# Moving the row scaling of the final norm to the end of the last expert, and the last down-projection block in two halves

## The chip, the cores and the metric

The kernel runs on one NeuronCore of a Trainium2 chip, as one program. The metric is the time of one execution on the device in microseconds (us). TensorE multiplies matrices into PSUM, VectorE and ScalarE work on tiles in SBUF and PSUM, GpSimd (POOL in the profile) does small operations and issues the indirect transfers, SyncE (SP) issues the plain transfers. A matmul in float32 precision is made of float32r products: each operand is split into a rounded high half and the low rest.

## The reference, cut to what matters

One layer of a diffusion backbone over 1024 latent tokens of 1024 channels. The change lies in its last part, a mixture of 16 experts and the final norm:

```
def expert_choice_ffn(h, w_router, w_gate, w_up, w_down):
    ...
    gates, idx = lax.top_k(jnp.swapaxes(aff, 1, 2), cap)      # cap = 128 tokens of each of 16 experts
    xe = jax.vmap(lambda hb, ib: hb[ib])(h, idx)
    hid = jax.nn.silu(jnp.einsum('becd,edf->becf', xe, w_gate)) * jnp.einsum('becd,edf->becf', xe, w_up)
    ye = jnp.einsum('becf,efd->becd', hid, w_down) * gates[..., None].astype(h.dtype)
    return jax.vmap(lambda yb, ib: jnp.zeros((n, d), yb.dtype).at[ib.reshape(-1)].add(yb.reshape(-1, d)))(ye, idx)
...
        x = x + gt2 * expert_choice_ffn(h, router_w[i], exp_w_gate[i], exp_w_up[i], exp_w_down[i])
    return rms_norm(x, final_g)
```

The root mean square of a token's row is taken over all its 1024 channels, so a row can be scaled only when every expert that chose the token has added to it.

## The kernel before, in words

The experts run one after the other. Each has 24 weight blocks of 512 by 512 (1 MB of float32): blocks 0 to 15 are gate and up (four hidden blocks of 512 channels, four weight blocks each), blocks 16 to 23 are the down projection, in the order of `DOWN` (L1214), (n2, kk) = (0,0), (0,1), (0,2), (1,0), (1,1), (1,2), (0,3), (1,3): n2 is the half of the 1024 output channels, kk the hidden block. So block 21 is (1,2), block 22 completes the first half of the output and block 23 the second.

`Stream.get` (L121) keeps weights ahead of the products: at block b it emits the split of block b+2. A split (L75, L76) is a cast of the raw block on ScalarE (`ewh`) and a subtraction on VectorE (`ewl`); the last two blocks are split in quarters of 512 columns. Three pairs of `ewh` and `ewl` exist, so the cast of block b+3 waits for the products of block b with its `ewh`. A block is 12 products of 512 columns: eight with `ewh`, four with `ewl` (`products`, L83).

PE, ScalarE and VectorE run in the order in which the program is written (`tc.manual_schedule`, L1714); SP and POOL are ordered by the framework. In that order block b does: the split of block b+2, the list `pre[b]`, the list `post[b]`, its products. What the lists hold for the last expert, whose block 0 is L:

- `hidden` (L1636), per hidden block: silu on ScalarE, multiply into `sge` on VectorE, four transposes on TensorE, and the split of the transposed block (`hd`: copy on ScalarE, subtraction on VectorE). For the last hidden block: silu in post 14, multiply in post 16, transposes in pre 18, split in post 18.
- `rows` (L1674, post 1) loads all 1024 rows of the residual stream as eight tiles of 128 tokens, once the scatter of the last but one expert is done. They hold every contribution but the last expert's.
- `row_sum(t)` (L1686, post 11+t): squares and sum of tile t on ScalarE; for every second t the reciprocal root for two tiles on POOL (`rstd_of`, L201).
- `row_out(t)` (L1692): VectorE scales tile t by the reciprocal root and the norm's weight `fg`, SP writes it to `out`. It stands in post 13, 14, 16, 17, 19, 20, 21 and 22.
- `last_rows(n2)` (L1696), for the 128 tokens of the last expert: the down projection's half times gate and `gt2` (`yl`), added to their rows (`xl`), squares summed on ScalarE (`ssl`), and times `fg` (`zl`). `last_rows(0)` stands in post 23, `last_rows(1)` behind block 23.

After the loop: the two sums added, the reciprocal root (L749, one step of it on POOL), `zl` scaled by it, the first half on VectorE and the second on ScalarE (L1751, L1752), and an indirect DMA on POOL's queue that scatters these 128 rows into `out` (L1753), over what `row_out` wrote for the same tokens.

Of the kernel before, what the change touches and what calls it, by code (L numbers as in the profile page):

```python
# [8 lines left out]
F32 = mybir.dt.float32  # L9
# [5 lines left out]
AF = mybir.ActivationFunctionType  # L15
OP = mybir.AluOpType
AX = mybir.AxisListType

D = 1024
# [8 lines left out]
NE = 16  # L28
CAP = 128
DE = 2048  # L30
EPS = 1e-6
# [4 lines left out]
def block_kernel(ctx: ExitStack, tc, x, c, cx, c_ctx, w_ada, b_ada, norm1_g, norm2_g, w_in, w_a_up, b_a,  # L36
# [3 lines left out]
    V, S, G, T = nc.vector, nc.scalar, nc.gpsimd, nc.tensor  # L40
# [18 lines left out]
    small = ctx.enter_context(tc.tile_pool(name="small", bufs=2))  # L59
# [11 lines left out]
    def ps(name="ps"):  # L71
        return psum.tile([128, 512], F32, name=name, tag="ps")
# [10 lines left out]
    def products(p, ab, w, first, last, again=False):  # L83

        seq = [q for a, b in ab for q in ((a[0], b[0]), (a[0], b[1]) if w == 0 else (a[1], b[0]))]
        seq += [(a[1], b[0]) if w == 0 else (a[0], b[1]) for a, b in ab]
        for i, (a, b) in enumerate(seq):
            T.matmul(p, a, b, start=first and i == 0, stop=last and i == len(seq) - 1, skip_group_check=again)  # L88
            yield

    def mmw(p, ab, w=0, first=True, last=True, again=False):
        for _ in products(p, ab, w, first, last, again):
            pass

    def drain(gen, n=None):

        i = 0
        while n is None or i < n:
            try:
                next(gen)  # L100
            except StopIteration:
                return True
            i += 1
        return False
# [93 lines left out]
    mhalf = const.tile([128, 8], F32, name="mhalf")  # L198
    V.memset(mhalf, -0.5)

    def rstd_of(dst, ssq, n, cols, eng=None):  # L201

        a = small.tile([128, cols], F32, name="rs_a", tag="rs_a", bufs=4)
        r = small.tile([128, cols], F32, name="rs_r", tag="rs_r", bufs=4)
        t = small.tile([128, cols], F32, name="rs_t", tag="rs_t", bufs=4)
        eng = eng or V
        eng.tensor_scalar(a, ssq, 1.0 / n, EPS, op0=OP.mult, op1=OP.add)  # L207
        G.tensor_tensor(r, a, mhalf[:, :cols], op=OP.pow)  # L208
        eng.tensor_mul(t, r, r)  # L209
        eng.tensor_mul(t, t, a)  # L210
        eng.tensor_scalar(t, t, -0.5, 1.5, op0=OP.mult, op1=OP.add)  # L211
        eng.tensor_mul(dst, r, t)  # L212
# [52 lines left out]
    def g4(name, dt=F32):  # L265
        return gw.tile([128, N], dt, name=name, tag="g4", bufs=GB)
# [78 lines left out]
    def ada_mm(j):  # L345
        p = ps()
        for k in range(KT):
            q = 32 * (k % 4)
            T.matmul(p[q:q + 32, :256], cS32[:, k], pairs[j][:, k], start=(k < 4), stop=(k >= 4))
        a = hpool.tile([128, 256], F32, name="ada", tag="A", bufs=2)  # L350
        V.tensor_copy(a, p[:, :256])
        return a
# [43 lines left out]
    xl, xl2 = [], []  # L396
    pv = [[ps() for hf in range(2)] for t in range(2)]
    plr = ps()
    for j in range(KT):
# [8 lines left out]
        if j + 1 < KT:  # L408
            a = ada_mm(j + 1)
        w = ws.get()  # L410
        for t in range(2):
            st = (hcT[j][0][:, t * 128:(t + 1) * 128], hcT[j][1][:, t * 128:(t + 1) * 128])
# [383 lines left out]
    for h in range(H):  # L796
# [33 lines left out]
        o = [g4("o0"), g4("o1")]  # L830
# [16 lines left out]
    for i in range(2):  # L847
        w = ws.get()
# [303 lines left out]
    for j in range(8):  # L1152
        w = ws.get()
# [32 lines left out]
    for f in range(2):  # L1186
# [3 lines left out]
        for j in range(8):  # L1190
            w = ws.get()
# [7 lines left out]
            hi, lo = mgX[j // 4][f]  # L1199
# [303 lines left out]
    while not drain(sg_, 1):  # L1503
# [27 lines left out]
                           op0=OP.add, op1=OP.mult)  # L1531
# [74 lines left out]
    gt2 = ep.tile([128, D], F32, name="gt2")  # L1606

    def spread(dst, c0):

        for n in range(2):  # L1610
            dg = ep.tile([128, 4, 128], F32, name="dg", tag="oh", bufs=1)
            for k in range(4):
                S.activation(dg[:, k], ident, AF.Copy, scale=mc[:, c0 + 4 * n + k:c0 + 4 * n + k + 1])
            yield
            p = ps()
            for k in range(4):
                T.matmul(p[:, k * 128:(k + 1) * 128], ones, dg[:, k], start=True, stop=True)
            yield
            S.copy(dst[:, n * 512:(n + 1) * 512], p)
# [7 lines left out]
    NB = 24  # L1627
    pre = [[] for _ in range(NE * NB + 2)]
    post = [[] for _ in range(NE * NB + 2)]

    def put(gen, *places):

        for where, b in places:
            where[b].append(lambda: drain(gen, 1))
# [33 lines left out]

    lt = {}
    ssq = small.tile([128, 8], F32, name="ssq3", bufs=1)  # L1670
    ssl = small.tile([128, 2], F32, name="ssl", bufs=1)
    rs = small.tile([128, 8], F32, name="rs3", bufs=1)

    def rows():  # L1674
# [11 lines left out]
    def row_sum(t):  # L1686
        sq = ep.tile([128, D], BF16, name="sq3", tag="oh", bufs=1)
        S.activation(sq, xs[t], AF.Square, accum_out=ssq[:, t:t + 1])  # L1688
        if t % 2:
            rstd_of(rs[:, t - 1:t + 1], ssq[:, t - 1:t + 1], D, 2, G)  # L1690

    def row_out(t):  # L1692
        V.scalar_tensor_tensor(xs[t], xs[t], rs[:, t:t + 1], lt["fg"], op0=OP.mult, op1=OP.mult)
        nc.sync.dma_start(out[t * 128:(t + 1) * 128, :], xs[t])

    def last_rows(n2, st):  # L1696

        gate, xl, zl, fg = tok[NE - 1][2], lt["xl"], lt["zl"], lt["fg"]
        h = slice(n2 * 512, (n2 + 1) * 512)
        yl = ep.tile([128, 512], F32, name="yl", tag="sge", bufs=2)  # L1700
        sq = ep.tile([128, 512], F32, name="sq4", tag="sge", bufs=2)
        V.scalar_tensor_tensor(yl, st["pd", n2], gate, gt2[:, h], op0=OP.mult, op1=OP.mult)
        V.tensor_tensor(xl[:, h], xl[:, h], yl, op=OP.add)
        S.activation(sq, xl[:, h], AF.Square, accum_out=ssl[:, n2:n2 + 1])
        V.tensor_tensor(zl[:, h], xl[:, h], fg[:, h], op=OP.mult)

    L = (NE - 1) * NB
    post[L + 1].append(rows)
    for t in range(8):
        post[L + 11 + t].append(lambda t=t: row_sum(t))  # L1710
        post[L + (13, 14, 16, 17, 19, 20, 21, 22)[t]].append(lambda t=t: row_out(t))
    put(spread(gt2, 16), (post, 9), (pre, 11), (post, 12), (pre, 14), (post, 15))

    with tc.manual_schedule(engines={mybir.EngineType.PE, mybir.EngineType.Activation, mybir.EngineType.DVE}):  # L1714
        for g in range(NE * NB):
            e, b = divmod(g, NB)
            if b == 0:
                st = {}
                for nb in range(4):
                    put(hidden(e, nb, st), (post, g + 4 * nb + 2), (post, g + 4 * nb + 4), (pre, g + 4 * nb + 6),  # L1720
                        (post, g + 4 * nb + 6))
                if e + 1 < NE:
                    put(gather(e + 1), (post, g + 4), (pre, g + 6), (post, g + 7))
                    pre[g + 17].append(lambda e=e: lt.update(ei=expert_in(e + 1)))
                    for w_, b_ in ((pre, 17), (post, 17), (pre, 20), (post, 20)):
                        w_[g + b_].append(lambda: drain(lt["ei"], 1))
                    put(expert_out(e, st), (post, g + 23), (post, g + 24))
                else:
                    post[g + 23].append(lambda st=st: last_rows(0, st))
            w = es.get()  # L1730
            for f in pre[g] + post[g]:
                f()
            if b < 16:
                nb, r = divmod(b, 4)
                nm = "pu" if r > 1 else "pg", nb
                if r % 2 == 0:
                    st[nm] = ps()
                mmw(st[nm], [(xT[e](4 * (r % 2) + k), w(k)) for k in range(4)], 1, r % 2 == 0, r % 2 == 1)
            else:
                n2, kk = DOWN[b - 16]  # L1740
                if kk == 0:
                    st["pd", n2] = ps()
                hi, lo = st["hd", kk]
                mmw(st["pd", n2], [((hi[:, k * 128:(k + 1) * 128], lo[:, k * 128:(k + 1) * 128]), w(k)) for k in range(4)],
                    1, kk == 0, kk == 3)
        last_rows(1, st)
    rl = small.tile([128, 1], F32, name="rl", bufs=1)
    V.tensor_add(ssl[:, 0:1], ssl[:, 0:1], ssl[:, 1:2])
    rstd_of(rl, ssl[:, 0:1], D, 1)
    zl = lt["zl"]  # L1750
    V.tensor_scalar(zl[:, :512], zl[:, :512], rl, None, op0=OP.mult)  # L1751
    S.activation(zl[:, 512:], zl[:, 512:], AF.Copy, scale=rl)  # L1752
    nc.gpsimd.indirect_dma_start(out=out[:, :], out_offset=bass.IndirectOffsetOnAxis(ap=tok[NE - 1][0][:, :1], axis=0),  # L1753
                                 in_=zl, in_offset=None)
    close(epc)
# [28 lines left out]
```

## Time and profile before

| | |
|---|---|
| time, median of 3 runs | 2319.63 us (2318.67 to 2321.66) |
| the profiled execution | 2319.61 us, its span 2317.8 us |
| TensorE busy | 2243.7 us, 97% of the span |
| VectorE busy | 1734.1 us, 75% |
| ScalarE busy | 1341.3 us, 58% |
| mean granted TensorE clock | 0.988 |

All times in rows are us from the start of the span. In a time line a row has start, duration, engine, line, operation, out<-in and the number of operations merged into it; in square brackets the idle time of the engine before it and what ended it. L75, L76 and L88 are lines of helpers, so the tile names tell the operation. In rows of groups the mean duration of one operation, in ns, stands behind the bar after the busy time. `eraw` is the name of all tiles of the weight ring; the rows of tokens and `zl` lie in such tiles too.

### The profile page before, as it was taken

What the parts mean: (1) busy time and instruction counts of PE and PEld (TensorE: products, weight loads), DVE (VectorE), ACT (ScalarE), POOL (GpSimd) and SP (SyncE); (2) the same over time, 40 slices, a digit from 0 to 9 for tenths busy, and PEclk for the clock granted to TensorE, in tenths of its full rate; (3) what the DMA queues carried; (4) which work ended last, traced back from release to release, by engine and by line L of the source; (5) the groups of instructions that cost most, each with busy time, mean ns of one, the idle gap of its engine ahead of it and who ended that gap; (6) DMA issues with size and microseconds to landing.
All of it is one profiled execution on the core that took longest, in us unless ns stands there. A gap on an engine that the chain in (4) does not pass through costs nothing. (4 is left out here: it accounts for less than half of the span.)

```text
span 2317.8 us, 28964 instructions
## 1 busy us (share of the span) xinstructions
PE 2243.7 (97%) x10930; PEld 1861.4 (80%) x10930; DVE 1734.1 (75%) x2183; ACT 1341.3 (58%) x1538; POOL 281.8 (12%) x388
## 2 busy tenths in 40 slices
PE   6999999999999999999959999999999999999997
PEld 4888888888788887888748888888888888888885
DVE  5764545454866665476688999999999999999988
ACT  3743433342333344253448777777777777777786
POOL 1201010101000023320210111100011101011104
PEclk9999999999999999999979999999999999999998
DMA  9423333334222258665579999999999999999995
GB/s 321 157 61 110 103 107 99 109 96 155 64 75 76 77 180 264 215 204 180 221 281 324 388 383 380 375 380 393 392 386 376 380 376 393 388 388 378 382 349 208
DMA packets 356341, 589.60 MB, mean 254 GB/s; under 512 B 15498, under 2 KB 122096, under 8 KB 356200
## 3 DMA queue, kind: packets, MB, share of 16 engines
q1 hardware_dynamic: 331664, 506.65, 61.3%
q0 software_dynamic: 24192, 80.86, 10.6%
q8 instruction: 85, 1.39, 0.2%
q14 instruction: 56, 0.46, 0.1%
q10 hardware_dynamic: 344, 0.24, 0.0%
HBM read 537.34 MB, written 50.35 MB: 254 GB/s over the span
## 5 line engine op out<-in xcount | busy, mean ns | idle before, releaser
L76 DVE TENSOR_TENSOR ewl<-eraw,ewh 128x2048 fp32r<-128x2048 f32 (+1 forms) x391 | 865.4, 2223 | 93.6 <-ACT ewh L75 89.4
L75 ACT CAST ewh<-eraw 128x2048 fp32r<-128x2048 f32 (+1 forms) x391 | 726.8, 1862 | 224.1 <-PE ps L88 220.0
L88 PE MATMUL ps<-ewh,xeh 128*128 128x512 f32 x1024 | 404.5, 395 | 0.3 <-ACT xeh L75 0.3
L88 PE MATMUL ps<-ewh,xel 128*128 128x512 f32 x1024 | 399.9, 391 | 0.0
L88 PE MATMUL ps<-ewl,xeh 128*128 128x512 f32 x1024 | 274.0, 389 | 0.0
L88 PE MATMUL ps<-ewh,hd 128*128 128x512 f32 x1024 | 259.6, 396 | 0.0
L88 PE MATMUL ps<-hTh,whi 128*128 128x512 f32 x596 | 237.6, 399 | 0.0
L88 PE MATMUL ps<-hTl,whi 128*128 128x512 f32 x596 | 232.3, 390 | 0.0
L88 PEld LDWEIGHTS ps<-ewl,xeh 128*128 128x128 f32 x1024 | 192.3, 188 | 40.3
L88 PEld LDWEIGHTS ps<-ewh,xeh 128*128 128x128 f32 x1024 | 192.8, 188 | 39.3 <-ACT xeh L75 0.7
L88 PEld LDWEIGHTS ps<-ewh,xel 128*128 128x128 f32 x1024 | 192.9, 188 | 38.9 <-DVE xel L76 0.2
L88 PEld LDWEIGHTS ps<-ewh,hd 128*128 128x128 f32 x1024 | 189.6, 189 | 37.8
L75 ACT CAST whi<-wraw 128x1024 fp32r<-128x1024 f32 (+1 forms) x97 | 87.6, 917 | 164.1 <-PE ps L88 122.4
L76 DVE TENSOR_TENSOR wlo<-wraw,whi 128x1024 fp32r<-128x1024 f32 (+1 forms) x97 | 101.3, 1057 | 101.2 <-ACT whi L75 55.0
L88 PE MATMUL ps<-hTh,wlo 128*128 128x512 f32 x596 | 152.5, 390 | 0.0
L88 PE MATMUL ps<-ewl,hd 128*128 128x512 f32 x512 | 137.5, 390 | 0.0
L1661 POOL DMA_INDIRECT x_d<-ye,idc x15 | 50.7, 3381 | 693.2 <-DVE ye L1660 693.2
L88 PEld LDWEIGHTS ps<-hTh,whi 128*128 128x128 f32 x596 | 112.0, 188 | 27.4 <-issue 2.6
L88 PEld LDWEIGHTS ps<-hTh,wlo 128*128 128x128 f32 x596 | 111.5, 188 | 23.5
L88 PEld LDWEIGHTS ps<-hTl,whi 128*128 128x128 f32 x596 | 112.0, 188 | 22.2
L88 PEld LDWEIGHTS ps<-ewl,hd 128*128 128x128 f32 x512 | 96.5, 188 | 20.5
L965 ACT COPY snap<-ps 128x512 f32<-128x512 f32 x59 | 34.7, 589 | 100.2 <-PE ps L88 96.3
(464 smaller groups left out, 3545.0 us busy)
## 6 DMA issues: line engine op xcount, KB each, us to landing
eraw<-in_exp_w_down_dram SPq DMA_DIRECT2D x128, 1024.0 KB
eraw<-in_exp_w_gate_dram SPq DMA_DIRECT2D x127, 1024.0 KB
eraw<-in_exp_w_up_dram SPq DMA_DIRECT2D x127, 1024.0 KB
wraw<-in_w_in_dram SPq DMA_DIRECT2D x76, 512.0 KB
raw<-in_w_ada_dram SPq DMA_DIRECT2D x64, 256.0 KB
adaw<-in_w_ada_dram SPq DMA_DIRECT2D x16, 512.0 KB
sig_d<-sgm POOLq DMA_DIRECT2D x32, 256.0 KB, 2.8
sgl<-sig_d POOLq DMA_DIRECT2D x32, 256.0 KB, 4.8
```

The costliest lines, as they stand in the source:

```text
L75: S.copy(hi, src)
L76: V.tensor_sub(lo, src, hi.bitcast(F32))
L88: T.matmul(p, a, b, start=first and i == 0, stop=last and i == len(seq) - 1, skip_group_check=again)
L965: S.copy(t, p)
L1661: nc.gpsimd.indirect_dma_start(out=x1_d[:, :], out_offset=bass.IndirectOffsetOnAxis(ap=idc[:, :1], axis=0), in_=ye, in_offset=None, comput ...
```

## The change

The eight `row_out` move: 0 to post 19, 1 to post 20, 2 and 3 to post 21, 4 and 5 to post 22, and 6 and 7 behind the scaling of `zl`, ahead of the scatter in the program. The products of the last block (1,3) are done in two halves of 256 columns, each with its own 12 products; `last_rows` handles the first 512 channels, then 256 and 256. The sum of the first two parts, with the mean and epsilon, is formed ahead of the third part. The last steps are inside the hand-ordered section, and their one-column values lie in a wider `ssl`.

```
-    ssl = small.tile([128, 2], F32, name="ssl", bufs=1)
+    ssl = small.tile([128, 8], F32, name="ssl", bufs=1)
+    sl0, ra, rr, rt, rl = (ssl[:, i:i + 1] for i in range(3, 8))
...
-    def last_rows(n2, st):
+    def last_rows(i, st):
...
-        h = slice(n2 * 512, (n2 + 1) * 512)
+        n2, o, w_ = ((0, 0, 512), (1, 0, 256), (1, 256, 256))[i]
+        h = slice(n2 * 512 + o, n2 * 512 + o + w_)
...
+        V.scalar_tensor_tensor(yl[:, :w_], st["pd", n2][:, o:o + w_], gate, gt2[:, h], op0=OP.mult, op1=OP.mult)
+        V.tensor_tensor(xl[:, h], xl[:, h], yl[:, :w_], op=OP.add)
+        S.activation(sq[:, :w_], xl[:, h], AF.Square, accum_out=ssl[:, i:i + 1])
         V.tensor_tensor(zl[:, h], xl[:, h], fg[:, h], op=OP.mult)
+        if i == 1:
+
+            V.tensor_add(sl0, ssl[:, 0:1], ssl[:, 1:2])
+            V.tensor_scalar(sl0, sl0, 1.0 / D, EPS, op0=OP.mult, op1=OP.add)
...
-        post[L + (13, 14, 16, 17, 19, 20, 21, 22)[t]].append(lambda t=t: row_out(t))
+        if t < 6:
+            post[L + (19, 20, 21, 21, 22, 22)[t]].append(lambda t=t: row_out(t))
...
+                if g == NE * NB - 1:
+                    for o in (0, 256):
+                        mmw(st["pd", n2][:, o:o + 256],
+                            [((hi[:, k * 128:(k + 1) * 128], lo[:, k * 128:(k + 1) * 128]), tuple(a[:, o:o + 256] for a in w(k)))
+                             for k in range(4)], 1, False, True, True)
+                    continue
...
-                    1, kk == 0, kk == 3)
+                    1, kk == 0, kk == 3 or g == NE * NB - 3)
         last_rows(1, st)
...
+        last_rows(2, st)
+        zl = lt["zl"]
+        V.tensor_scalar(ra, ssl[:, 2:3], 1.0 / D, sl0, op0=OP.mult, op1=OP.add)
+        G.tensor_tensor(rr, ra, mhalf[:, :1], op=OP.pow)
+        V.tensor_mul(rt, rr, rr)
+        V.tensor_mul(rt, rt, ra)
+        V.tensor_scalar(rt, rt, -0.5, 1.5, op0=OP.mult, op1=OP.add)
+        V.tensor_mul(rl, rr, rt)
+        V.tensor_scalar(zl[:, :512], zl[:, :512], rl, None, op0=OP.mult)
+        S.activation(zl[:, 512:], zl[:, 512:], AF.Copy, scale=rl)
+        row_out(6)
+        row_out(7)
```

## Rows read from the trace of the kernel before

**Rows 1.** Time line of TensorE: transposes of the last hidden block, block 18, block 23.

```profile
2285.97 0.66 PE L1645 MATMUL ps<-ident,sge 128*128 128x128 f32 x4 [2.08 <-DVE sge L1641]
2286.38 3.42 PE L88 MATMUL ps<-ewh,hd 128*128 128x512 f32 x8
...
2301.67 1.98 PE L88 MATMUL ps<-ewh,hd 128*128 128x512 f32 x8
```

**Rows 2.** Time line of VectorE from the last `sge` multiply to `last_rows(0)`.

```profile
2285.23 0.68 DVE L1641 TENSOR_TENSOR sge<-ps,sge 128x512 f32<-128x512 f32 x1
...
2292.03 2.28 DVE L76 TENSOR_TENSOR ewl<-eraw,ewh 128x2048 fp32r<-128x2048 f32 x1
2294.23 1.28 DVE L1693 SCALAR_TENSOR_TENSOR eraw<-eraw,rs,eraw 128x1024 f32<-128x1024 f32 x1
2295.42 2.49 DVE L76 TENSOR_TENSOR ewl<-eraw,ewh 128x512 fp32r<-128x512 f32 x4
...
2301.44 2.47 DVE L1693 SCALAR_TENSOR_TENSOR eraw<-eraw,rs,eraw 128x1024 f32<-128x1024 f32 x2
2303.83 0.74 DVE L1702 SCALAR_TENSOR_TENSOR yl<-ps,ig,gt 128x512 f32<-128x512 f32 x1
```

**Rows 3.** Windows: stretch, length, busy per engine, granted clock, DMA share, GB/s.

```profile
2285.97:2290.79 4.82, 4.82 (x17) 3.89 (x17) 4.82 (x3) 2.88 (x5) 4.65 (x3) 0.65 0.40 164
```

**Rows 4.** Time line of all engines, the last steps.

```profile
2305.94 0.74 DVE L1702 SCALAR_TENSOR_TENSOR yl<-ps,ig,gt 128x512 f32<-128x512 f32 x1
...
2308.04 0.19 ACT L1704 ACTIVATION_READ_ACCUMULATOR sq<-xl 128x1 f32 x1
...
2308.45 0.15 DVE L207 TENSOR_SCALAR rs_a<-ssl 128x1 f32<-128x1 f32 x1
...
2310.04 0.48 DVE L1751 TENSOR_SCALAR eraw<-eraw,rl 128x512 f32<-128x512 f32 x1
2310.04 0.72 ACT L1752 ACTIVATE eraw<-eraw,rl 128x512 f32<-128x512 f32 x1 [1.82 <-DVE rl L212]
2311.34 1.05 POOL L1753 DMA_INDIRECT out_dram<-eraw,idc  x1 [2.10 <-ACT eraw L1752]
```

**Rows 5.** Lines L1753 (last scatter) and L1661 (fifteen scatters): waits, landing.

```profile
L1753 POOLq EVENT_SEMAPHORE  x5: 17/43/1604, 2308.6 to 2309.0; - x5
...
DMA to landing us min/median/max: 3.4/3.4/3.4
...
L1661 POOLq EVENT_SEMAPHORE  x2: 17/30/43, 1228.2 to 1228.3; - x2
```

**Rows 6.** Time line of ScalarE: casts of units 18, 20, 21, the `hd` copy.

```profile
2278.76 1.93 ACT L75 CAST ewh<-eraw 128x2048 fp32r<-128x2048 f32 x1
...
2284.46 1.91 ACT L75 CAST ewh<-eraw 128x2048 fp32r<-128x2048 f32 x1
...
2287.30 0.59 ACT L75 CAST hd<-ps 128x512 fp32r<-128x512 f32 x1
2289.83 1.91 ACT L75 CAST ewh<-eraw 128x2048 fp32r<-128x2048 f32 x1 [1.94 <-PE ps L88]
```

**Rows 7.** Operations of 256 columns: a time line row, then groups by form.

```profile
101.16 0.64 PE L88 MATMUL ps<-wlo,hTh 128*128 128x256 f32 x4
...
L658 DVE SCALAR_TENSOR_TENSOR sf<-sf,rc,ps 128x256 f32<-128x256 f32 x24 | 11.5, 480 | 38.2 <-PE ps L655 37.9
...
L693 DVE TENSOR_TENSOR A<-az,az 128x256 f32<-128x256 f32 x16 | 6.8, 423 | 0.5
...
L723 ACT ACTIVATE sqo<-o 128x256 bf16<-128x256 f32 x32 | 13.3, 417 | 1.0
```

**Rows 8.** Windows of 0.5 us (columns as in rows 3): where transfers end.

```profile
2306.00:2306.50 0.50, 0.00 (x0) 0.00 (x0) 0.50 (x2) 0.05 (x1) 0.00 (x0) 1.00 0.08 25
...
2314.00:2314.50 0.50, 0.00 (x0) 0.00 (x0) 0.00 (x0) 0.00 (x0) 0.00 (x0) 0.50 0.40 156
```

**Rows 9.** DMA issues: queue, count, KB each, median us from issue to landing.

```profile
x_d<-side POOLq DMA_DIRECT2D x6, 512.0 KB, 4.1
```

More of the change, by code (lines that the diff above doesn't have):

```diff
@@ L1694, in row_out @@
         nc.sync.dma_start(out[t * 128:(t + 1) * 128, :], xs[t])
-    def last_rows(n2, st):
+    def last_rows(i, st):
         gate, xl, zl, fg = tok[NE - 1][2], lt["xl"], lt["zl"], lt["fg"]
-        h = slice(n2 * 512, (n2 + 1) * 512)
+        n2, o, w_ = ((0, 0, 512), (1, 0, 256), (1, 256, 256))[i]
+        h = slice(n2 * 512 + o, n2 * 512 + o + w_)
         yl = ep.tile([128, 512], F32, name="yl", tag="sge", bufs=2)
         sq = ep.tile([128, 512], F32, name="sq4", tag="sge", bufs=2)
-        V.scalar_tensor_tensor(yl, st["pd", n2], gate, gt2[:, h], op0=OP.mult, op1=OP.mult)
-        V.tensor_tensor(xl[:, h], xl[:, h], yl, op=OP.add)
-        S.activation(sq, xl[:, h], AF.Square, accum_out=ssl[:, n2:n2 + 1])
+        V.scalar_tensor_tensor(yl[:, :w_], st["pd", n2][:, o:o + w_], gate, gt2[:, h], op0=OP.mult, op1=OP.mult)
+        V.tensor_tensor(xl[:, h], xl[:, h], yl[:, :w_], op=OP.add)
+        S.activation(sq[:, :w_], xl[:, h], AF.Square, accum_out=ssl[:, i:i + 1])
         V.tensor_tensor(zl[:, h], xl[:, h], fg[:, h], op=OP.mult)
+        if i == 1:
+            V.tensor_add(sl0, ssl[:, 0:1], ssl[:, 1:2])
+            V.tensor_scalar(sl0, sl0, 1.0 / D, EPS, op0=OP.mult, op1=OP.add)
     L = (NE - 1) * NB
@@ L1743, in block_kernel @@
                 hi, lo = st["hd", kk]
+                if g == NE * NB - 1:
[4 more added lines that the diff above has]
+                    continue
                 mmw(st["pd", n2], [((hi[:, k * 128:(k + 1) * 128], lo[:, k * 128:(k + 1) * 128]), w(k)) for k in range(4)],
-                    1, kk == 0, kk == 3)
+                    1, kk == 0, kk == 3 or g == NE * NB - 3)
         last_rows(1, st)
[L1747 to L1752, printed above, removed]
+        last_rows(2, st)
[10 more added lines that the diff above has]
+        row_out(7)
     nc.gpsimd.indirect_dma_start(out=out[:, :], out_offset=bass.IndirectOffsetOnAxis(ap=tok[NE - 1][0][:, :1], axis=0),
```

## The prediction

> **What bounds the kernel now.** I read the busy shares of the page first: TensorE is busy for 97% of the span and VectorE for 75%, so over the whole run products set the time. The change touches only the last expert, so I then read that stretch in the time lines of each engine and in windows, from about 2270 us on. There the picture is another one.
>
> TensorE stands still for 2.08 us after its block 17, because the four transposes of the last hidden block wait for VectorE's `sge` multiply [rows 1], and that multiply starts only at 2285.23 [rows 2]: VectorE has done the rows of other tokens (row_out 0, 1 and 2, three times 1.2 us) ahead of it. Behind the gap the granted clock is 0.65 over the next block [rows 3], so part of that block runs at the lower of the two levels, 1.2 instead of 2.4 GHz: its eight matmuls of the high half take 3.42 us [rows 1], where those of the last block take 1.98.
>
> But TensorE is not what comes last. Its last block begins at 2301.67 and ends near 2304.5 [rows 1], while VectorE is without a pause from 2285 on: splits, row_out 4 to 7, and only at 2303.83 the first operation of `last_rows(0)` [rows 2], although block 22, which it reads, was through at about 2301.8. From there one chain leads to the end: `last_rows(0)`, `last_rows(1)` at 2305.94, the statistics, the scaling of `zl` at 2310.04, the scatter at 2311.34 [rows 4], its landing 3.4 us later [rows 5], and some 3 us of closing drains. I call the start of the `zl` scaling Z (2310.04 before), the start of `last_rows(0)` D0 (2303.83 before). What delays Z or what stands between Z and the scatter is paid in full.
>
> **Part 1: row_out 0 to 3 leave the blocks 13 to 17.** VectorE loses four operations there, 1.19 us each (2.39 for two [rows 2]). What is late next? The ScalarE cast. ScalarE works through casts and `row_sum`s back to back up to the `hd` copy at 2287.30 [rows 6]; nothing in the change touches that order, and no VectorE result holds it up there. So VectorE now follows the casts: the cast of unit 18 ends at 2280.69 [rows 6], its split (2.20 from start to start) runs to 2282.9, the `sge` multiply to 2283.6. TensorE comes to the transposes at 2283.9 (2285.97 less the 2.08 [rows 1]), so the gap closes and with it the slow block: TensorE gets back 2.1 us of gap and about 1.7 us of slow clock (3.42 less 1.98, and the four products behind them), some 3.8 us, and ends its last block near 2300.7.
>
> VectorE gets back less. The cast of unit 20 ends at 2286.37 and the `hd` copy at 2287.89 [rows 6]; the cast of unit 21 no longer waits 1.94 us for TensorE, so it runs from 2287.8 to 2289.7. The split of unit 21 then starts at 2289.7 instead of 2292.03 [rows 2]: 2.3 us earlier. Between 2274 and that point VectorE idles about 2.6 us waiting for casts: most of the time that the four rows leave free is not usable.
>
> **Part 2: six rows in the last four blocks instead of four.** From the split of unit 21 on, VectorE's list is: split 2.20, row 1.19, split in quarters 2.41 (2.49 long, the next operation starts 0.08 before its end), row 1.20, split in quarters 2.41 [rows 2], then row_out 2 to 5, four times 1.20 = 4.80. Sum 14.2 us, from 2289.7: D0 = 2303.93. Before: 2303.83. So two more rows behind the split of unit 21 (2.4 us) eat the 2.3 us: +0.1 us. Bounds: if VectorE never waited for a cast after 2274, D0 would come 2.7 us earlier; if TensorE's gap stayed and the cast of unit 21 with it, 2.1 us later. I take +0.1, as every wait in it is read off a cast that stays where it is.
>
> **Part 3: the last block in halves of 256 columns.** 24 products instead of 12, each with its weight load. Products of 256 columns follow each other every 0.12 us (four in 0.64, the last one 0.28 long [rows 7]), so the block takes 2.9 instead of 2.7 us. Nobody waits: VectorE reaches `last_rows(1)` near 2306.0, five us after TensorE's end. For the same reason the halving brings nothing: it would let VectorE start on the first half early, and VectorE isn't there.
>
> What it costs is the split of `last_rows(1)` in two. `last_rows(0)` keeps its 2.11 us [rows 2, 4]. For a half I take the nearest rows of 256 columns: 0.48 for the operation from PSUM, 0.42 for a tensor_tensor, 0.42 for ScalarE's squares and 0.19 for the read of its accumulator [rows 4, 7]. In order, counted from D0: yl 2.11, xl 2.62, zl 3.07; ScalarE's sum is there at 3.64; the add 3.67 and the tensor_scalar 3.86 (both new places, 0.19 each); second half yl 4.03, xl 4.54 to 4.96, ScalarE's sum at 5.53; `ra` at 5.56; from there to Z 1.59 as before (2308.45 to 2310.04 [rows 4]). Z = D0 + 7.15; before it was D0 + 6.21. That is +0.94 us. Bounds: halves at half the price of 512 columns give +0.3, halves as dear as 512 give +2.1; the 256-column rows lie near the lower side, so 0.94 stands. With part 2, Z comes 1.04 us later, at 2311.08.
>
> **Part 4: row_out 6 and 7 behind the scaling.** On VectorE they follow the `zl` scaling (0.48, the next starts 0.40 after it): row 6 from Z+0.40, row 7 from Z+1.60 to Z+2.88. Each issues a write of 512 KB into `out` on SP's queue. The scatter writes rows of the same `out`, so it has to come after them, and the trace says that it is held: five semaphore waits stand in front of it on POOL's queue, against two in front of all fifteen scatters into x1 together [rows 5]. Before, they cost nothing since the last row write was long in place: row 7 was done on VectorE at 2303.83 and its bytes were through early in the slice from 2306.00 [rows 8]. The scatter's own bytes end 0.4 us before its landing (share 0.40 of the slice from 2314.00 [rows 8], landing at 2311.34 + 3.4 [rows 4, 5]), so I take a landing at 2306.5, 2.7 us after VectorE's end. Then row 7 lands at Z+5.58, and the scatter starts 0.6 us behind that (0.58 from ScalarE's end to its start [rows 4]): Z+6.2, where before it was Z+1.30. That is +4.9 us. Bounds: 4.3 if the wait is over with the last byte and the start comes at once, 6.3 if the write takes the 4.1 us that 512 KB writes took on POOL's queue earlier in the kernel [rows 9].
>
> The Trainium skill, "DMA: Bandwidth & Descriptors", section "Anatomy of one DMA", prices a transfer at a fixed 2.0 us and its bytes at 436 GB/s, which for 512 KB is an estimate of 3.2 us from issue to landing. The scatter's 3.4 us agree with it, and the SP write's 2.6 us (0.1 after VectorE's end to the landing) don't. By the page the sum would be 0.6 us more; the measurement decides.
>
> **No cost.** The `stop` flag on block 21 changes no instruction's work. The statistics in columns of `ssl` are the same operations on other addresses. Dropping the tile `rl` moves everything allocated behind it by one small tile; I take nothing for it, since no row ties a duration to a place (the last rival has the other end).
>
> **Sum.** +0.1 +0.94 +4.9 = +5.9 us. The profiled execution took 2319.61 us (span 2317.8, 1.8 around it), the median of the runs is 2319.63, so no correction: 2325.5 us. By the parts' nearer bounds its own range is 2324.0 to 2327.3.
>
> **Rivals.**
> - *The scatter doesn't wait for the rows.* Then it starts at Z+1.3 and only Z's +1.04 is paid: 2320.7 us; row 7 lands 1.5 us after the scatter would start to write, before the closing drains. For it: the five waits are not named in the trace. Against: nothing else on SP's queues needs waiting for at that point, and the write would be lost to the row beneath it. Chance 0.08.
> - *VectorE keeps up, and TensorE sets the end* (the other side: not slower). Place: D0. If the row operations found room so that `last_rows(0)` and the first half were done by TensorE's end at 2300.7, the second half would start at 2300.8, Z would be 3.1 us later (7.15 less 4.03) at 2303.9, the scatter at 2310.1, 1.2 us earlier than now: 2318.4 us. It decides from D0 below about 2298.5. For it: TensorE's 3.8 us are real. Against: 14.2 us of VectorE work stand behind a cast that can't end before 2289.7. Chance 0.07. With the first rival as well the scatter would start at 2305.2: 2313.5 us, chance 0.03.
> - *TensorE's gap stays.* If the `sge` multiply slips behind something and TensorE again waits near 2 us, the cast of unit 21 is late as before, and the two more rows are paid in full: D0 +2.1, time 2327.6. For it: the multiply is done only 0.3 us before TensorE needs it. Against: a miss of a few tenths makes no 2 us. Chance 0.08.
> - *The moved tiles cost something everywhere.* Half a per cent would be 11 us: 2336. Nothing in the trace speaks for it. Chance 0.03.
>
> My forecast has the remaining 0.71, a tenth of it between 2322.5 and 2324.2. What a measurement of this kernel can tell from no change is 0.2%, 4.6 us: above 2324.3 counts as slower, below 2315.0 as faster. Slower: 0.60 of the forecast's 0.71, and the two rivals behind it (0.08, 0.03), together 0.70. Within: the rest of the forecast and the first two rivals, 0.26. Faster: 0.04. The range takes in the first rival and the third, 2320.4 to 2328.0, and leaves out the second, the pair and the last.
>
> **What would show it.** In the trace of after: no TensorE gap near 2284 and a clock of 1.00 in block 18; TensorE's end near 2300.7; four rows on VectorE back to back and the first yl near 2303.9; Z near 2311.1; two row operations after the scaling, and about 6 us from Z to the scatter, ended by a wait on a DMA into `out`. It is wrong if yl starts well before 2303, if the scatter starts within 2 us of Z, or if the blocks ahead of the last expert differ.

## The result, and the profile after

The changed kernel takes 2357.48 us (2355.09 to 2358.61, 4 runs) against 2319.15 (2317.98 to 2321.66, 4 runs) of the kernel before: a ratio of 1.0169 [1.0156, 1.0182], 38.3 us slower. The prediction was 2325.5, with a range up to 2328.0. The direction was right and the size was not, and most of the loss lies where the prediction looked at nothing.

The first view after the time is where the loss lies. I take an event that both kernels have ahead of the change's place, the issue of the last expert's last `up` block, and count from it. Before, it stands at 2232.32 us of the span (D0, 2303.83 [rows 2], is 71.51 behind it); after, at 2263.93:

```profile
2232.32 0.37 SPq L1243 DMA_DIRECT2D eraw<-in_exp_w_up_dram  x1
```

```profile
2263.93 0.37 SPq L1243 DMA_DIRECT2D eraw<-in_exp_w_up_dram  x1
```

So 31.6 of the 39.0 us between the spans (2317.8 and 2356.8) are there before any moved instruction runs. Only 7.4 us arise in the end. The delay builds up along the whole run: it is 8.6 us when the first expert's first `up` loads into the weight ring are issued (1169.02 us before, 1177.58 after), and from expert to expert it then grows by some 1.6 us.

In that stretch TensorE does nothing but products in both kernels. Windows from inside the experts, the kernel before and then the one after (columns as in [rows 3]):

```profile
1270.00:2230.00 960.00, 960.00 (x4490) 795.12 (x4490) 881.08 (x562) 754.15 (x589) 83.22 (x28) 1.00 1.04 383
```

```profile
1278.00:2260.00 982.00, 982.00 (x4487) 795.19 (x4487) 882.01 (x562) 751.24 (x590) 84.47 (x28) 1.00 1.03 375
```

TensorE is never idle in either, the granted clock is 1.00 in both, and the weights, which come at 375 instead of 383 GB/s, do not keep TensorE waiting. About as many matmuls, 4490 and 4487, take 960 and 982 us: each takes longer on average. The groups by form say which. Kernel before (out<-in, shapes, count, busy us, mean ns of one, idle before):

```profile
L88 PE MATMUL ps<-ewh,xeh 128*128 128x512 f32 x1024 | 404.5, 395 | 0.3 <-ACT xeh L75 0.3
L88 PE MATMUL ps<-ewl,xeh 128*128 128x512 f32 x1024 | 274.0, 389 | 0.0
L88 PE MATMUL ps<-hTl,whi 128*128 128x512 f32 x596 | 232.3, 390 | 0.0
L80 PE MATMUL ps<-mwl,mgh 128*128 128x512 f32 x128 | 50.0, 390 | 0.0
L88 PE MATMUL ps<-ogh,whi 128*128 128x512 f32 x128 | 49.8, 389 | 0.0
L88 PE MATMUL ps<-cvh,wlo 128*128 128x512 f32 x128 | 31.8, 389 | 0.0
```

The same groups of the kernel after:

```profile
L88 PE MATMUL ps<-ewh,xeh 128*128 128x512 f32 x1024 | 410.2, 401 | 0.3 <-ACT xeh L75 0.3
L88 PE MATMUL ps<-ewl,xeh 128*128 128x512 f32 x1024 | 280.7, 395 | 0.0
L88 PE MATMUL ps<-hTl,whi 128*128 128x512 f32 x596 | 232.6, 390 | 0.0
L80 PE MATMUL ps<-mwl,mgh 128*128 128x512 f32 x128 | 50.5, 395 | 0.0
L88 PE MATMUL ps<-ogh,whi 128*128 128x512 f32 x128 | 49.8, 389 | 0.0
L88 PE MATMUL ps<-cvh,wlo 128*128 128x512 f32 x128 | 32.6, 395 | 0.0
```

Four of the six groups are 5 to 6 ns longer, two are unchanged to a nanosecond. The time line shows what that is worth per block. Before, the `ewl` part of one block and of the next:

```profile
1485.97 1.07 PE L88 MATMUL ps<-ewl,xeh 128*128 128x512 f32 x4
...
1488.69 1.07 PE L88 MATMUL ps<-ewl,xeh 128*128 128x512 f32 x4
```

After:

```profile
1500.09 1.10 PE L88 MATMUL ps<-ewl,xeh 128*128 128x512 f32 x4
...
1502.89 1.10 PE L88 MATMUL ps<-ewl,xeh 128*128 128x512 f32 x4
```

A block of 12 products takes 2.80 instead of 2.72 us: 0.2333 instead of 0.2267 us a product, 2.9% more. A block with four transposes in it grows less, 3.20 to 3.23 us. Some 18 of an expert's 24 blocks have no transposes between their products: 18 times 0.08 and 6 times 0.03 us are the 1.6 us per expert.

What sets the two kinds of groups apart is where their operands lie. SBUF is given out from two ends, in the code the pools of side "left" and of side "right". `ewh`, `ewl`, `hT..`, `mw..`, `whi`, `wlo` are on the left, behind the pool `small`; `xeh`, `xel`, `hd`, `mg..`, `cv..` on the right. The change takes the tile `rl` out of `small`, and the wider `ssl` still fits in the 32 bytes that it had, so everything on the left behind `small` starts 32 bytes lower (`xp` at 22496 instead of 22528 bytes in a partition) and nothing on the right moves. In the kernel before, all these tiles start at multiples of 256 bytes. In the large groups, products with one operand on each side got slower, and products with both on one side, as `hTl,whi`, did not. The runs below are on this.

The end of the kernel after, VectorE and then TensorE (to compare with [rows 1, 2, 4]):

```profile
2322.07 2.29 DVE L76 TENSOR_TENSOR ewl<-eraw,ewh 128x2048 fp32r<-128x2048 f32 x1 [0.43 <-ACT ewh L75]
...
2331.49 4.87 DVE L1694 SCALAR_TENSOR_TENSOR eraw<-eraw,rs,eraw 128x1024 f32<-128x1024 f32 x4
2336.27 0.76 DVE L1704 SCALAR_TENSOR_TENSOR yl<-ps,ig,gt 128x512 f32<-128x512 f32 x1
...
2343.73 0.49 DVE L1768 TENSOR_SCALAR eraw<-eraw,ssl 128x512 f32<-128x512 f32 x1
2344.13 2.48 DVE L1694 SCALAR_TENSOR_TENSOR eraw<-eraw,rs,eraw 128x1024 f32<-128x1024 f32 x2
```

```profile
2316.65 0.60 PE L1645 MATMUL ps<-ident,sge 128*128 128x128 f32 x4
2317.00 2.10 PE L88 MATMUL ps<-ewh,hd 128*128 128x512 f32 x8
...
2333.45 0.63 PE L88 MATMUL ps<-ewl,hd 128*128 128x256 f32 x4
```

The gap ahead of the transposes is gone and the eight products behind them take 2.10 instead of 3.42 us [rows 1]. TensorE ends at 2334.1, but the first `yl` starts at 2336.27, behind four rows in one piece. From Z (2343.73) the scatter is 6.56 us away. The view of the line of the row writes (L1695) names the scatter as waiting for them. The scatter's own row of POOL's time line names no releaser (`issue`), so run 8 has to confirm it. The third fence is the window in which the last row's bytes end:

```profile
L1695 SPq DMA_DIRECT2D out_dram<-eraw x8: 332/332/357, 2325.6 to 2346.6; - x8
...
  POOL out_dram L1772: 7.4, 1
```

```profile
2350.29 1.05 POOL L1772 DMA_INDIRECT out_dram<-eraw,idc  x1 [7.37 <-issue]
```

```profile
2348.50:2349.00 0.50, 0.00 (x0) 0.00 (x0) 0.00 (x0) 0.00 (x0) 0.00 (x0) 0.50 0.51 205
```

### The profile page after: what moved, and what is told of

Its sections match the earlier page's. It is cut to its first block, busy times and chain, and to the rows that moved or that the text cites. A ratio compares the mean times of both kernels' runs of the same rounds, so it can differ in the third digit from the quotient of the medians.

```text
span 2356.8 us, 28992 instructions
## 1 busy us (share of the span) xinstructions
PE 2276.4 (97%) x10942; PEld 1861.6 (79%) x10942; DVE 1736.5 (74%) x2187; ACT 1340.2 (57%) x1540; POOL 279.4 (12%) x388
## 5 line engine op out<-in xcount | busy, mean ns | idle before, releaser
L88 PE MATMUL ps<-ewh,xeh 128*128 128x512 f32 x1024 | 410.2, 401 | 0.3 <-ACT xeh L75 0.3
L88 PE MATMUL ps<-ewh,xel 128*128 128x512 f32 x1024 | 405.0, 396 | 0.0
L88 PE MATMUL ps<-ewl,xeh 128*128 128x512 f32 x1024 | 280.7, 395 | 0.0
L88 PE MATMUL ps<-ewh,hd 128*128 128x512 f32 (+1 forms) x1032 | 263.3, 397 | 0.0
L88 PE MATMUL ps<-ewl,hd 128*128 128x512 f32 (+1 forms) x516 | 140.5, 394 | 0.0
L1661 POOL DMA_INDIRECT x_d<-ye,idc x15 | 50.7, 3381 | 707.7 <-DVE ye L1660 707.7
```

Source lines behind the costliest of these rows:

```text
L1661: nc.gpsimd.indirect_dma_start(out=x1_d[:, :], out_offset=bass.IndirectOffsetOnAxis(ap=idc[:, :1], axis=0), in_=ye, in_offset=None, comput ...
```

## The experiments

Ratios are to runs of the kernel before on the same chip, with a 95% interval; differences in us are between medians. That kernel's median was 2317.67 for the first four runs, 2316.42 for the next four, 2317.57 for the last three.

**Run 1 (e1): the change with its old addresses.** The kernel after, with an unused tile in `rl`'s place.

```
     rs = small.tile([128, 8], F32, name="rs3", bufs=1)
+    small.tile([128, 1], F32, name="pad2", bufs=1)
```

> The changed kernel with one unused 32-byte tile in the pool `small`, so that every tile behind it lies where it lay before the change. Theory A (TensorE's two operands must lie alike: the tile `rl` gone moved the weight tiles 32 bytes against the activations and made each product of 512 columns 0.2333 us instead of 0.2267): the step is 0.2267 again, the expert stage is as long as before, and only the predicted end is left: 2325 to 2327 us. Rival B (the slow products come from something else in the change, such as its other instructions): the step stays at 0.233 and the time near 2357 us.

Measured: 2324.25 us (2320.95 to 2326.75), ratio 1.0036 [1.0022, 1.005], +6.6 us. `ewl,xeh` is back at 390 ns. One unused tile of 4 bytes in a partition takes back some 32 us, and what is left is the end that the prediction had worked out as +5.9 (the interval of the ratio is 5 to 12 us).

**Run 2 (e2): the addresses without the change.** The kernel before, with `rl` as a column of `ssl`.

```
-    ssl = small.tile([128, 2], F32, name="ssl", bufs=1)
+    ssl = small.tile([128, 8], F32, name="ssl", bufs=1)
...
-    rl = small.tile([128, 1], F32, name="rl", bufs=1)
+    rl = ssl[:, 7:8]
```

> The kernel before with one edit: the value `rl` lies in a column of `ssl`, which is the same size in memory, so the pools behind `small` on its side lie 32 bytes lower; no instruction changes. Theory A: a step of 0.2333 us in the expert stage and some 31 us more, 2350 us. Rival B: 2319 us, step 0.2267.

Measured: 2352.78 us (2351.44 to 2354.41), ratio 1.0156 [1.0141, 1.0172], +35.1 us; `ewl,xeh` at 396 ns. Runs 1 and 2 split the change in two: the order and the halves cost 6.6, the place some 32 to 35.

**Run 3 (e3): both sides moved.** Run 2, and the right side moved by 32 bytes as well. This tells apart whether an address of its own must be a multiple of something or only the distance between the two operands.

```
-    top.tile([128, 56], F32, name="pad")
+    top.tile([128, 64], F32, name="pad")
```

> As the run before, and the pools of the other side (activations, hidden blocks, most of the weight ring) 32 bytes lower too, so that both operands of a product lie alike again, though neither on a multiple of 64 or 256 bytes. Theory A (only the distance between the two operands counts): step 0.2267, time 2319 to 2321 us. Rival C (each operand has to lie on a multiple of 64 bytes or more for itself): step 0.233 or more, 2350 us or slower.

Measured: 2318.94 us (2316.6 to 2320.04), ratio 1.0007 [0.9997, 1.0016]. Nothing clear of noise is left of the 35 us, though now neither operand of those products lies where it lay before. So it is the distance that counts, and not either address for itself. The one group in the kernels of runs 1, 2, 3 and 5, in this order:

```profile
L88 PE MATMUL ps<-ewl,xeh 128*128 128x512 f32 x1024 | 274.1, 390 | 0.0
```

```profile
L88 PE MATMUL ps<-ewl,xeh 128*128 128x512 f32 x1024 | 281.1, 396 | 0.0
```

```profile
L88 PE MATMUL ps<-ewl,xeh 128*128 128x512 f32 x1024 | 274.2, 390 | 0.0
```

```profile
L88 PE MATMUL ps<-ewl,xeh 128*128 128x512 f32 x1024 | 274.2, 389 | 0.0
...
L88 PE MATMUL ps<-cvh,wlo 128*128 128x512 f32 x128 | 32.6, 395 | 0.0
...
L88 PE MATMUL ps<-t3l,whi 128*128 128x512 f32 x60 | 23.8, 396 | 0.0
```

The same group in runs 4, 6 and 7, in this order (in run 7 the helper's line is L87):

```profile
L88 PE MATMUL ps<-ewl,xeh 128*128 128x512 f32 x1024 | 280.3, 395 | 0.0
```

```profile
L88 PE MATMUL ps<-ewl,xeh 128*128 128x512 f32 x1024 | 280.2, 395 | 0.0
```

```profile
L87 PE MATMUL ps<-ewl,xeh 128*128 128x512 f32 x1024 | 274.3, 390 | 0.0
```

**Run 4 (e4): 64 bytes.** The kernel before, its left side 64 bytes lower (this moves the pools `const` and `small` too).

```
-    const.tile([128, 40], F32, name="pad")
+    const.tile([128, 24], F32, name="pad")
```

> The kernel before with the first pool's padding 64 bytes smaller, so that all pools of that side lie 64 bytes lower against the other side. Theory A with a period of 64 bytes: step 0.2267, 2319 to 2321 us. Theory A with a longer period (128 or 256 bytes), or rival D (transfers into the weight ring want multiples of 256 bytes): 2335 to 2355 us; in the first case the products' step is longer, in the second TensorE waits with the step at 0.2267.

Measured: 2347.67 us (2345.52 to 2351.96), ratio 1.0141 [1.0125, 1.0156]; `ewl,xeh` at 395 ns. For the experts' products 64 bytes are as slow as 32. `cvh,wlo` is at 392 here, between its fast 389 and its slow 395.

**Run 5 (e5): only the experts' right side follows.** Run 2, and the pools of the right side that hold `xeh`, `xel` and `hd` moved by 32 bytes; the pool of `cv..` and `mg..` stays.

```
-    rp.tile([128, 56], F32, name="pad")
+    rp.tile([128, 64], F32, name="pad")
```

> The kernel before moved by 32 bytes as in e2, and of the other side only the pools opened last (`sp` with the hidden blocks, `ep` with the experts' activations, one ring tile) moved by 32 bytes too; the pool `yp` with the earlier stages' activations and 8 of 14 weight ring tiles stays. Theory A (distance between the two operands of one product): the expert stage has its step of 0.2267 us back, while products of the earlier stages that pair the two sides keep their slow step; in e2 those cost 8.6 us up to the first expert, so 2326 us. Rival C' (what counts is where the weight ring lies against the tiles that the casts write, or where transfers land): the expert stage stays at 0.233 and the time at 2352 us.

Measured: 2327.35 us (2326.02 to 2327.57), ratio 1.0048 [1.0033, 1.0064]. Group by group the time goes with the pair: `ewl,xeh` is at 389 ns again, while `cvh,wlo` stays at 395 in the same execution (the fourth fence under run 3). One execution holds both kinds, so the state of the chip in one run can't be behind it. Of the 10.9 us that stay, the groups that the trace still shows slow explain nearly all: 384 products with `cv..`, 384 with `mw..`, 180 of `hTh,w` and `hTl,w` and 540 with `t1..` to `t3..` (`t3l,whi` is at 396, before at 389) are 1488 times at most 6.7 ns, up to 10 us.

**Run 6 (e6): 128 bytes.** As run 4, with `[128, 8]` in place of `[128, 24]`.

> The kernel before with the first pool's padding 128 bytes smaller, so that the one side lies 128 bytes lower against the other. At 32 and at 64 bytes the step was 0.233. If the operands' distance counts with a period of 128 bytes: 0.2267 and 2318 to 2321 us. If with 256 bytes or more: 0.230 to 0.234, 2340 to 2355 us.

Measured: 2349.98 us (2348.73 to 2353.16), ratio 1.0149 [1.0134, 1.0165]; `ewl,xeh` at 395 ns.

**Run 7 (e7): a distance of 256 bytes.** Run 2 without the tile `pad` of `top`, which puts the right side 224 bytes off and the distance between the sides 256 bytes from that of the kernel before.

```
-    top.tile([128, 56], F32, name="pad")
```

> The kernel before with one side 32 bytes lower and the other 224 bytes higher, a distance changed by 256 bytes. Period of at most 256 bytes: step 0.2267, 2318 to 2321 us. A longer period, or each place counting for itself at this distance: 0.23 and 2340 us or more.

Measured: 2318.39 us (2316.45 to 2323.23), ratio 1.0013 [1.0004, 1.0022]; `ewl,xeh` at 390 ns. So shifts of 32, 64 and 128 bytes are slow, 0 and 256 fast, and the three slow ones cost nearly the same (35.1, 30.0 and 33.6 us). The interval of run 7 lies 1 to 5 us above the kernel before, which these products don't show. Other distances weren't tried.

**Run 8 (e9): no row behind the end.** Run 1 with all eight rows ahead of `last_rows(0)`; the halves stay.

```
-        if t < 6:
-            post[L + (19, 20, 21, 21, 22, 22)[t]].append(lambda t=t: row_out(t))
+        post[L + (14, 15, 19, 20, 21, 21, 22, 22)[t]].append(lambda t=t: row_out(t))
...
-        row_out(6)
-        row_out(7)
```

> The changed kernel with the place kept as in e1, and all eight row operations ahead of the end (blocks 14, 15, 19, 20, 21, 21, 22, 22); the halves stay. In e1 from the scaling of `zl` to the scatter 6.56 us passed instead of 1.30, which I put down to the wait for the writes of rows 6 and 7. By that theory the scatter follows 1.3 us after the scaling again; rows 0 and 1 fall into VectorE's waits for casts, so the first yl stays at most 0.5 us later than before, and the halves cost 1.2 us: 1.2 to 2 us over the kernel before, 5 us under e1. Rival (the scatter is held by something else at the end, such as its place in POOL's queue): 6 us from scaling to scatter again.

Measured: 2317.93 us (2314.88 to 2322.91), ratio 1.0006 [0.9997, 1.0015], +1.5 us. The transposes and the last products on TensorE, then the end on all engines:

```profile
2280.75 0.66 PE L1645 MATMUL ps<-ident,sge 128*128 128x128 f32 x4 [0.68 <-DVE sge L1641]
...
2297.26 0.64 PE L88 MATMUL ps<-ewl,hd 128*128 128x256 f32 x4
```

```profile
2307.58 0.49 DVE L1768 TENSOR_SCALAR eraw<-eraw,ssl 128x512 f32<-128x512 f32 x1
2308.88 1.05 POOL L1770 DMA_INDIRECT out_dram<-eraw,idc  x1 [2.10 <-ACT eraw L1769]
```

The scatter is at Z+1.30 again, as before the change [rows 4], and the 5 us are gone. What stays in the trace is the price of the halves (Z − D0 is 7.45 instead of 6.21); the time alone can't show so little.

**Run 9 (e10): no halves either.** The kernel before with the rows in the places of run 8. The kernel that ran also forms the first half of `zl` in one operation at the end instead of two, an edit that its expectation does not count:

```
-        V.tensor_tensor(zl[:, h], xl[:, h], fg[:, h], op=OP.mult)
+        if n2:
+            V.tensor_tensor(zl[:, h], xl[:, h], fg[:, h], op=OP.mult)
...
-    V.tensor_scalar(zl[:, :512], zl[:, :512], rl, None, op0=OP.mult)
+    V.scalar_tensor_tensor(zl[:, :512], lt["xl"][:, :512], rl, lt["fg"][:, :512], op0=OP.mult, op1=OP.mult)
```

> The kernel before with only the row operations moved, to blocks 14, 15, 19, 20, 21, 21, 22, 22: TensorE's gap is gone, the last block is whole. My theory of the end (VectorE is the late engine, TensorE's 3.8 us are worth nothing alone; the halves cost 1.2 us): the first yl within 0.5 us of before against the last transfers of weights, the scaling of `zl` 6.21 us behind it, time within 1 us of before. Rival (TensorE sets the end): 3 to 4 us less than before.

Measured: 2317.08 us (2314.39 to 2318.68), ratio 0.9997 [0.9988, 1.0006]. In its trace TensorE's gap is 0.68 us, the next block has no slow clock, and TensorE's end is 3 us earlier against the common event (69.26 behind it instead of 72.23). D0 is where it was (71.62 and 71.51). So the 3 us are real and buy nothing: the rows that left the earlier blocks stand in front of `last_rows(0)`. The event, VectorE around D0, and TensorE's transposes and last products:

```profile
2227.23 0.37 SPq L1243 DMA_DIRECT2D eraw<-in_exp_w_up_dram  x1
```

```profile
2294.07 4.87 DVE L1697 SCALAR_TENSOR_TENSOR eraw<-eraw,rs,eraw 128x1024 f32<-128x1024 f32 x4
2298.85 0.75 DVE L1706 SCALAR_TENSOR_TENSOR yl<-ps,ig,gt 128x512 f32<-128x512 f32 x1
```

```profile
2279.48 0.66 PE L1645 MATMUL ps<-ident,sge 128*128 128x128 f32 x4 [0.68 <-DVE sge L1641]
...
2295.42 1.07 PE L88 MATMUL ps<-ewl,hd 128*128 128x512 f32 x4
```

The scaling does not come 6.21 us behind D0, as expected, but 5.69: this is the edit of `zl`. Its operation at the end is longer for it (0.75 us instead of 0.48), and the scatter comes 7.26 behind D0 instead of 7.51. So the time compares the moved rows less 0.25 us; D0, which the edit can't touch, is the cleaner sign.

**Runs 10 and 11 (e11, e12): rows taken off VectorE.** If VectorE's list sets the end, rows on other engines should shorten it. Run 9, with rows 6 and 7 (run 10) or 4 to 7 (run 11) done by ScalarE and GpSimd in post 21 (in run 10 row 5 goes to post 22). The edit of run 10, where run 11 has `(4, 5, 6, 7)`; other rows stay on VectorE:

```
+        if t in (6, 7):
+            S.activation(xs[t], xs[t], AF.Copy, scale=rs[:, t:t + 1])
+            G.tensor_tensor(xs[t], xs[t], lt["fg"], op=OP.mult)
```

> As e10, and VectorE loses work: rows 6 and 7 are scaled on ScalarE in block 21 (idle there) and multiplied by `fg` on GpSimd, and the first half of `zl` is formed in one operation at the end instead of two. By my theory VectorE's lateness is the time: the first yl comes 2.4 us earlier, the scaling another 0.6 us, so 2.5 to 3 us under the kernel before. Rival (GpSimd's large operations hold VectorE up, or end too late for the scatter): no gain, or slower by some us.

> As e11 with rows 4 to 7 on ScalarE and GpSimd. By my theory VectorE is then ahead, the second half waits for TensorE's last product, and the time is 4 to 5 us under the kernel before, if GpSimd is through with four rows some 3 us ahead of the scatter. Rival (GpSimd is too slow for four): the scatter waits for the last row write, and the time is that of e11 or more.

Measured: run 10 2317.5 us (2315.96 to 2320.46), ratio 0.9999 [0.999, 1.0008]; run 11 2319.45 (2317.38 to 2322.76), ratio 1.0012 [1.0003, 1.0021]. No gain. Run 10's rival was right in its first half: GpSimd's operations hold VectorE up, and D0 comes 2.0 us later instead of 2.4 us earlier (73.54 behind the event; run 11: 73.37). The scatter doesn't wait for a row write in either run: it starts 1.57 us behind the scaling in both, as in run 9. So run 11's rival had the time right and the reason wrong. VectorE and GpSimd in run 11:

```profile
2287.92 2.49 DVE L76 TENSOR_TENSOR ewl<-eraw,ewh 128x512 fp32r<-128x512 f32 x4
...
2291.53 9.03 DVE L76 TENSOR_TENSOR ewl<-eraw,ewh 128x512 fp32r<-128x512 f32 x4
2300.48 0.74 DVE L1706 SCALAR_TENSOR_TENSOR yl<-ps,ig,gt 128x512 f32<-128x512 f32 x1
2301.25 2.06 DVE L1707 TENSOR_TENSOR xl<-xl,yl 128x512 f32<-128x512 f32 x1
```

```profile
2291.62 11.14 POOL L1695 TENSOR_TENSOR eraw<-eraw,eraw 128x1024 f32<-128x1024 f32 x4
```

The same split in quarters takes 2.49 us without GpSimd and 9.03 beside its four multiplications; TensorE then waits for its last weights (1.93 and 2.25 us). Run 10 has the small form of it, 4.70 us for the split beside two multiplications. Beside GpSimd's last one, `yl`, which takes one of its inputs from PSUM, keeps its 0.74 us, while `xl`, with two inputs from SBUF, takes 2.06 instead of 0.69. The Trainium skill, "SBUF — State Buffer", section "SBUF: two separate sides", says that VectorE and GpSimd share a pair of ports which one of them holds for its whole instruction, when VectorE reads two inputs from SBUF; these rows agree with it.

No version here beats the kernel before.

## Why the prediction was right and wrong, step by step

**The step that failed** is "No cost": for the dropped tile `rl` it took nothing, "since no row ties a duration to a place". What it measured is 35.1 us alone (run 2), and in the kernel after 31.6 us ahead of the last expert's last `up` load. In its place the runs show products of 512 columns that take 0.2333 instead of 0.2267 us each, because one operand moved against the other. The last rival had the mechanism in its heading, moved tiles that cost something everywhere, with 11 us and a chance of 0.03: the place right, the size a third of it. The prediction's argument was that no row speaks for it, but the profile of the kernel before could not show it, since the operands of these groups all start at multiples of 256 bytes there. What could have been read is in the code: four unused tiles named `pad` (in `const`, `top`, `gpool` and `rp`). A tile that nothing reads is most likely there for the addresses behind it, and the change moved those of one side. The rival should have had a real chance, and a price from TensorE's side: 2243.7 us of products on the path, of which each per cent is 22 us.

**D0, +0.1.** In run 1, with the old addresses, D0 stands 71.62 us behind the common event instead of 71.51: +0.11. The reasoning that VectorE follows ScalarE's casts holds, down to the wait in the trace of after (0.43 us for the cast of unit 21).

**Z − D0, +0.94.** Run 1 has 7.44 instead of 6.21, +1.23; the kernel after +1.25, run 8 +1.24. It lies inside the bounds of 0.3 and 2.1. The operations on the halves cost what their rows said (0.48, 0.42). What was mis-sized is the last sum: in run 1 ScalarE's squares of the last part start 0.38 us behind the end of `xl`, where those of the part before start 0.1 behind, so the sum is there at D0 + 5.76 instead of 5.53. No row says what held them.

**The scatter behind the rows, +4.9.** Measured +5.27 (run 1) and +5.26 (after), inside 4.3 to 6.3. From VectorE's end, 2346.61, to the scatter are 3.68 us; I had 3.3. The write itself was sized right: its bytes end near 2348.75 (0.51 of the slice shown above), which with the prediction's 0.4 us is a landing at 2349.2, where it had Z + 5.58, 2349.3. The scatter then starts 1.1 us behind the landing instead of 0.6. The lower bound was added up wrongly: if the wait is over with the last byte and the start comes at once, the term is 2.88 + 2.2 − 1.30 = 3.8, and 4.3 is the landing with a start at once. The measured value is above both. The range of the parts, 2324.0 to 2327.3, does not come out of the bounds named either (0.1 + 0.3 + 4.3 and 0.1 + 0.94 + 6.3 give 2324.3 and 2327.0), and the shares for slower add up to 0.71 instead of 0.70; nothing rests on these two. The first rival, a scatter that doesn't wait, is refuted by the 6.56 us from the scaling to the scatter together with run 8, where they are 1.30 without the two rows.

**The sum of the end** is then +6.6 by the terms of run 1 and +6.6 by its time, against 5.9 predicted. That terms and time agree so closely is in part luck, since the interval of the time is 5 to 12 us. In the kernel after the end cost 7.4: the other 0.8 are the last expert's own slow products. Run 2, which has no other change, shows 0.7 of it: its scatter starts 79.76 us behind the common event, before 79.02.

**The gap and its slow block.** Both went, as said: clock 1.00 in the block behind the transposes, eight products 2.10 instead of 3.42 us. That they bring nothing was the argument that TensorE isn't last. Run 9 shows it: D0 stays while TensorE ends 3 us earlier, and the ratio is 0.9997 [0.9988, 1.0006]. This also answers the second rival: D0 would have to come 5 us earlier for TensorE to set the end, and moving rows within VectorE's list does not do that.

**What stays open.** That the distance between the two sides' operands decides, and that 256 bytes more are as good as none while 32, 64 and 128 are not, is shown for this kernel's products of 512 columns. That it repeats every 256 bytes is not shown, with one such distance tried. Why it matters is not shown either: no row shows the reads of the two operands. These runs also can't tell the two operands of one product from the moving operand of one product and the weights that are loaded for the next, since both pairs lie alike in a block. One small group does not fit: `lrx,wa` (16 products) has both operands in one pool and goes from 394 to 396 ns in run 2. What distances other than those tried would cost, below 32 bytes or between 128 and 256, is not known.

## What to carry to other kernels

A tile that comes or goes moves the tiles allocated behind it on its side: where TensorE is the bound, compare the mean duration of the commonest product groups before you look for waits, and if some groups got slower and others not, according to the pools of their operands, put an unused tile in the gap and run again. An engine that stands idle for 2 us near the end is worth something only if it is last, so count the list of the engine that finishes behind it. And a write into the tensor that the last write goes to belongs ahead of the closing chain: behind it, two rows of 1.2 us each held the last scatter up by 5.3 us.

## What was not expected of the hardware

A product of 512 columns with its weight load follows the one before it in 0.2267 us when its two operands lie at the kernel's usual distance in a partition or 256 bytes off it, and in about 0.2333 us when the distance is 32 bytes off; 64 and 128 bytes off give the same mean durations for the experts' products (395 against 390 ns), at an unchanged granted clock of 1.00. Blocks that have transposes between their products lose less (3.20 to 3.23 us), and the `ewh,hd` products of 256 columns in the last block lose nothing (281 ns in the kernel after, 282 in run 1). And a GpSimd multiplication of 128x1024 takes 2.7 to 2.8 us (5.50 for two, 11.14 for four), in which VectorE's operations with two inputs from SBUF take up to 3.6 times as long (9.03 for 2.49).
